# A new issue order table for a four-layer hybrid decoder trunk on one core

## The chip, the cores and the metric

The kernel runs on one core of one Trainium2 chip. The metric is the device time of one execution in microseconds (us), lower is better. Three executions of the kernel before took 2624.12, 2625.46 and 2626.32 us; the median is 2625.46.

## The reference: what is computed

Four layers on 1024 positions of width 1024, float32, causal. Each layer adds a gated branch to the stream x:

```python
for i in range(DEPTH):                       # DEPTH = 4
    mod = (c @ ada_w[i] + ada_b[i])[:, None, :]
    shift, scale, gate = jnp.split(mod, 3, axis=-1)
    h = rmsnorm(x, norm_g[i]) * (1.0 + scale) + shift
    y = (hgrn2_mixer, swa_mixer, gdn_mixer)[i % 3](h, ...)
    x = x + gate * y
```

Layers 0 and 3 are HGRN2 (a gated linear recurrence, 8 heads of 128), layer 1 is attention in a window of 128 positions (16 query heads of 64, 4 key heads, a learned sink per head, rotary angles), layer 2 is a gated DeltaNet. The DeltaNet projects h to q and k (8 heads of 128), v and z (16 heads of 128) and two decay columns; q, k and v go through a causal convolution of four taps and a SiLU; then comes a recurrence over chunks, in which each head keeps a 128 x 128 state S:

```python
X = triangular_solve(A + eye, rhs)           # A = (k*beta) k^T * decay, below the diagonal
u, w = X[..., :dv], X[..., dv:]
v_new = u - w @ S
o = (q * exp(d)) @ S + (q k^T * dec) @ v_new
S = S * exp(d_last) + (k * exp(d_last - d))^T @ v_new
```

Every mixer ends with a norm per head, a SiLU gate from z, and an output projection.

## The kernel before: tiles, stages and what sets the order

The layers follow each other in time: layer 0 to about 600 us, attention to about 1075, the DeltaNet to about 2050, layer 3 and the store to the end. The stream is held as 1024 channels (8 tiles of 128 partitions) by two halves of 512 positions.

**Projections.** All big products run in three passes of a split float32: weights and activations are each a high part and a remainder, and `mm3` (L346 ff.) issues hi x hi (L350), lo x hi (L351, activation remainder) and hi x lo (L352, weight remainder), 128 x 512 outputs each, 24 matmuls per projection tile. `load_w` brings a weight block by a DMA on SP's queue into a buffer of the tag "raw" (three of them), ScalarE casts the high part (L321, scaled L324), VectorE takes the remainder (L322, scaled L325). Projection tiles lie in a PSUM pool "proj" of two buffers, and a pool "ta" beside it.

**Conditioning.** The shift, scale and gate of the next layer are worked out as a side stream (`ada`, L574 to L602): blocks ada_w come by DMA into the same three raw buffers, VectorE multiplies and adds them into ada_acc (L574, L576), transposes (L594) and reduces it (L595), TensorE adds over partitions (L598), and VectorE adds the bias into mod (L602). What needs the next layer's h, or the attention's last part behind it on VectorE, comes after L602.

**Attention.** Per head group: transposes of q (qt_ps, L1609), a split of it (L1613 on ScalarE, L1614 on VectorE), scores (s_ps, L1624 to L1626), the softmax (L1628 to L1641 on VectorE), the product with v (L1653), the gate (L1593, L1659).

**DeltaNet.** Its heads go in eight units of one key head and two value heads each. For each projection tile `conv` (L811 to L833) has ScalarE read the PSUM tile twice, a plain copy (L820) and a copy scaled by one tap (L824), then three taps on VectorE (L826), a tanh on ScalarE and the last product on VectorE (L833). q and k are transposed (`trans`, L839, four matmuls into qtr_ps or ktr_ps) and their squares summed by four ScalarE reads of that (L846). z is gated on VectorE from PSUM (L917, L918). `inverse` makes the triangular inverse of a unit: kk and qk products (L937, L938), a substitution loop on VectorE (L973, L974), a transposed copy through memory (L979, L984, L985), products z_ps (L1002 to L1031). `scan` is the recurrence of a unit, eight steps one after the other. A step is

1. ks_ps (L1070, L1071): the state S against k and against q;
2. gd_y on VectorE (L1076), one per value head, and a scaled copy on ScalarE (L1077);
3. w_ps (L1081), one per head, and gd_ws on ScalarE (L1082);
4. S_ps (L1086), and the new state gd_S on VectorE (L1092);
5. gd_wg on ScalarE (L1096), w_ps again (L1097), and the output's sum on VectorE (L1100).

TensorE's part is short, and the steps wait for small results of the other engines. So the recurrence of one unit stands among projections, convolutions and the inverse of later units, from about 1235 to 1890 us. The DeltaNet's outputs are normed and sent out in `finish` (L1041 to L1055).

**What sets the order.** The program is written as generators that are woven together (`weave`), which fixes each instruction and what it depends on. What stands in which place of each engine's queue is then fixed by a table, ORDER: for TensorE, ScalarE, VectorE, SP and GpSimd a packed list of numbers, one per instruction, 14230, 2952, 5663, 1353 and 378 of them. `in_order`, called at the end of `trunk`, takes at each number n the n-th instruction that is still left in program order, and ties it behind the one taken before. Each engine's queue runs strictly in that order; between engines the true dependences hold.

Of the kernel before, what the change touches and what calls it, by code (L numbers as in the profile page):

```python
# [33 lines left out]
GB = {"k": 5, "q": 4, "kt": 4, "v": 4, "tmp": 2, "tb": 4, "of": 2, "f256": 4, "ot": 1}  # L34
# [22 lines left out]
        "iwx`sRaG)%n;9&`wg^-}vk$8Bfgq(0bLMh`yeg$%91-I{rUNP*(qh<haKcQxkV{%berc<`?^bC8mnktaaK)n6P-wjm0si<P%K!qk2Da%1?*4"
        "An?NWr!m2{}31KUZv=7zYm#0n7FkwWAJKJv<FU$*rR1Y$l&LkV(=fdH7&3R{-D?1%xkBgAe>EF{iV4cVksXahUemcK-DwyTEBfhHV|>b`*@h"
        "(v;AK47(7bq^Z2-|N-)iDKPJsYQoESY#w(6+4}`T+J!$L+1B)nMJTXniy^e24!WWepY@31A3StZI=YOPX^Q9V_^0$P(4b0^)G#ZEDhtQ2F_<"
        "cG=TpmAx$(I#m}#<uC}FZVC$letO2R2s1gZPXtdy2f<fwWt`WzVQp@badQg3y@7f$P=`;y-guJk)K>1Kutp?M$-Gq(~`{%lK>+t9r0A$p%`S"  # L60
        "-s9@MWRu3*lw@+(u9j@0qPsleHEZg&Sr=je={Q!-a4XNnf4%j&|X{h1^B_q@$(<Z@>MvIf;P1dtrWF{eFP1_<eW}?l}|OdmyJD@81uLu)r6$"
        "Zru1fa`oz6xC6HVzJ{c8d;%YT49a6~(eTxpO7Q_5-jjlVLOgo(C|x6%hdn$^(ly+>_c1(zpX2X2gll&{Jp`r)yc;rUq8Zf6$_l{J+R`tUK3I"
        "CJo>P_6wR{z!^G$|tUAuN|b#)a!f~Qa6i6KI%)o!`??6cj-vuEkYJCMr^&KZ^+Q#i%LhjR}e%+0~9<K85~Q<4i8E&yytPM<z=nlTkPJ39+I-"
        "(&#j-QQ+l7lMy>0!+iy6s4qMBu@&#x-7r5e0h19<ss~6MY04$7h1TA$4{QX@wMX*kHfL|5rDIZ-3;&DyO+J4IW_<3=cM*eK2?vNo_=!r!_#Y"
        "P_NSdg=;frHQ%H{H`v86h?`xIcm#W@>7tX^uKyjS0`vr3K3PO$i4aBco+)Rg3vM5?woKwkPWRP;qOUkNvLWiJj>qi{PzJfpxgOl<^qOY${Y}"
        "-D>Le~K&DpAlw2R7PkYQSi1m6(8|#}U6r*nJ3a@CgwoO+{MRyx<&s3V}(OVE&0vmYp`bNu@^dZ)|KVm2w6^W@f0|2~5-8?)a2_jC|A5(vr7W"
# [1728 lines left out]
```

## Time and profile before

| | |
|---|---|
| median of three executions | 2625.46 us (2624.12 to 2626.32) |
| the profiled execution | 2630.06 us |
| its span in the trace | 2628.4 us |
| mean granted TensorE clock | 0.988 |
| DMA | 312.07 MB, mean 119 GB/s |
| GpSimd's busiest group, sends of o_in (L1450) | 72 of 539 ns |

The page names engines PE (TensorE), PEld (its weight loads), DVE (VectorE), ACT (ScalarE), POOL (GpSimd) and SP. A group row gives line, engine, operation, output and inputs, count, busy time, mean of one, and the idle time before with its releaser. A wait row names who waited, at which line, for whose result; then us in all, times, and the longest. In a row of a stretch come its length, the busy time and the instructions of each engine, the granted TensorE clock (1.00 is full), the DMA share and GB/s. A 128 x 512 matmul is shown with a length of 0.39 us, but the next starts 0.23 us after it, since they overlap: so a busy share near 100% still holds short stalls, and they are read from the waits and the starts.

### The profile page before, as it was taken

The numbers are of one execution on the slowest core, as the hardware profiler recorded it, in microseconds if no ns is written. First come the engines' busy times: TensorE is split into PE (matmuls) and PEld (weight loads), VectorE is DVE, ScalarE is ACT, GpSimd is POOL, SyncE is SP. The second block draws the span as 40 slices with busy tenths as digits, with TensorE's granted clock in tenths as the row PEclk, the third lists the DMA queues.
The fourth block names the chain that finished last, engine by engine and source line by source line (L and its number), as shares of the span: only waits on it lengthen the run. The fifth ranks groups of instructions, "written<-read, shape, count | busy, mean of one in ns | idle before, by whom it ended". The sixth has DMA issues, their size and how long they took to land.

```text
span 2628.4 us, 50793 instructions
## 1 busy us (share of the span) xinstructions
PE 2542.7 (97%) x18271; PEld 2058.0 (78%) x18271; DVE 2014.9 (77%) x5663; ACT 1328.7 (51%) x3480; POOL 164.7 (6%) x382
## 2 busy tenths in 40 slices
PE   7999999999999999999999999999999999999999
PEld 4777887788988877787777788778788877788877
DVE  5585789886787868678889989888776846468775
ACT  4444344543465656455566666565644534344452
POOL 0001000001000000100011101100222000000000
PEclk8999999999999999999999999999999999999999
DMA  7333444644233343444344344333576412122443
GB/s 262 99 112 106 129 128 122 192 126 141 69 97 97 112 138 102 133 110 111 86 111 115 90 124 114 88 85 90 164 239 199 133 37 84 51 85 66 139 146 117
DMA packets 393618, 312.07 MB, mean 119 GB/s; under 512 B 74979, under 2 KB 320150, under 8 KB 393366
## 3 DMA queue, kind: packets, MB, share of 16 engines
q1 hardware_dynamic: 380822, 267.92, 34.5%
q0 software_dynamic: 12544, 40.90, 4.9%
q8 instruction: 144, 2.36, 0.4%
q14 instruction: 108, 0.88, 0.1%
HBM read 247.84 MB, written 60.88 MB: 117 GB/s over the span
## 4 chain that ended last, share of the span: by engine, by line
PE 80%; DVE 7%; DMA 6%; issue 4%; ACT 3%; SPq 0%; POOL 0%; DVEq 0%; ACTq 0%; POOLq 0%
PE proj_ps L350 12%; PE proj_ps L351 12%; PE proj_ps L352 12%; PE outp_ps L350 4%; PE outp_ps L351 4%; PE outp_ps L352 4%; PE projw_ps L352 2%; PE projw_ps L351 2%; PE projw_ps L350 2%; DMA ada_w<-in_ada_w_dram 2%; PE projt_ps L350 2%; PE projt_ps L351 2%; PE projt_ps L352 2%; PE lev_ps L1253 1%; PE pv_ps L1653 1%
## 5 line engine op out<-in xcount | busy, mean ns | idle before, releaser
L350 PE MATMUL proj_ps<-hhi,w_hi 128*128 128x512 f32 x1664 | 677.0, 407 | 16.4 <-ACT gd_tb L824 9.9
L352 PE MATMUL proj_ps<-hhi,w_lo 128*128 128x512 f32 x1664 | 673.4, 405 | 0.0
L351 PE MATMUL proj_ps<-hlo,w_hi 128*128 128x512 f32 x1664 | 672.1, 404 | 0.0
L350 PEld LDWEIGHTS proj_ps<-hhi,w_hi 128*128 128x128 f32 x1664 | 315.2, 190 | 80.2 <-ACT gd_tb L824 15.6
L352 PEld LDWEIGHTS proj_ps<-hhi,w_lo 128*128 128x128 f32 x1664 | 315.1, 189 | 58.2 <-issue 1.6
L351 PEld LDWEIGHTS proj_ps<-hlo,w_hi 128*128 128x128 f32 x1664 | 315.4, 190 | 56.7 <-issue 1.4
L321 ACT CAST w_hi<-w_raw 128x512 fp32r<-128x512 f32 x356 | 216.5, 612 | 266.2 <-PE proj_ps L351 150.9
L322 DVE TENSOR_TENSOR w_lo<-w_raw,w_hi 128x512 fp32r<-128x512 f32 x356 | 238.7, 675 | 129.6 <-ACT w_hi L321 124.0
L350 PE MATMUL outp_ps<-o_hi,w_hi 128*128 128x512 f32 x576 | 228.4, 398 | 1.6 <-ACT o_hi L1458 1.0
L351 PE MATMUL outp_ps<-o_lo,w_hi 128*128 128x512 f32 x576 | 229.5, 399 | 0.1
L352 PE MATMUL outp_ps<-o_hi,w_lo 128*128 128x512 f32 x576 | 228.8, 398 | 0.1
L324 ACT ACTIVATE w_hi<-w_raw,par 128x512 fp32r<-128x512 f32 (+1 forms) x136 | 94.5, 697 | 142.4 <-PE outp_ps L351 84.8
L826 DVE SCALAR_TENSOR_TENSOR gd_tb<-gd_xs,taps,gd_tb 128x512 f32<-128x512 f32 x192 | 146.0, 760 | 13.2 <-ACT gd_tb L824 12.4
L576 DVE SCALAR_TENSOR_TENSOR ada_acc<-ada_w,par,ada_acc 128x512 f32<-128x512 f32 x154 | 115.2, 748 | 35.1 <-DMA ada_w<-in_ada_w_dram 34.4
L350 PEld LDWEIGHTS outp_ps<-o_hi,w_hi 128*128 128x128 f32 x576 | 108.7, 189 | 25.0 <-issue 2.5
L325 DVE SCALAR_TENSOR_TENSOR w_lo<-w_raw,par,w_hi 128x512 fp32r<-128x512 f32 (+1 forms) x136 | 97.4, 718 | 39.9 <-ACT w_hi L324 39.5
L351 PEld LDWEIGHTS outp_ps<-o_lo,w_hi 128*128 128x128 f32 x576 | 108.9, 189 | 23.1 <-DVE o_lo L1459 1.5
L352 PEld LDWEIGHTS outp_ps<-o_hi,w_lo 128*128 128x128 f32 x576 | 108.9, 189 | 22.4 <-issue 0.9
L1450 POOL DMA_DIRECT2D o_in<-od x72 | 38.8, 539 | 1183.2 <-DVE sw_zs L1593 321.0
L350 PE MATMUL projw_ps<-w_hi,hhi 128*128 128x512 f32 x256 | 101.6, 402 | 2.4 <-DVE hg_q L1169 2.3
L351 PE MATMUL projw_ps<-w_lo,hhi 128*128 128x512 f32 x256 | 102.5, 402 | 0.0
L352 PE MATMUL projw_ps<-w_hi,hlo 128*128 128x512 f32 x256 | 102.4, 402 | 0.0
(431 smaller groups left out, 5386.3 us busy)
## 6 DMA issues: line engine op xcount, KB each, us to landing
ada_w<-in_ada_w_dram SPq DMA_DIRECT2D x160, 256.0 KB, 2.8
w_raw<-in_hg_in_w_dram SPq DMA_DIRECT2D x148, 256.0 KB, 2.9
w_raw<-in_gd_in_w_dram SPq DMA_DIRECT2D x128, 256.0 KB, 3.0
o_in<-od POOLq DMA_DIRECT2D x72, 256.0 KB, 3.6
x<-xd SPq DMA_DIRECT2D x64, 256.0 KB, 4.8
w_raw<-in_gd_out_w_dram SPq DMA_DIRECT2D x64, 256.0 KB, 3.2
xd<-x POOLq DMA_DIRECT2D x48, 256.0 KB, 2.7
w_raw<-in_sw_in_w_dram SPq DMA_DIRECT2D x44, 256.0 KB, 3.0
```

Of the source, the lines that this page charges most:

```text
L321: nc.scalar.copy(hi, raw)
L322: nc.vector.tensor_tensor(lo, raw, hi.bitcast(F32), ALU.subtract)
L324: nc.scalar.activation(hi, raw, AF.Copy, scale=scale)
L325: nc.vector.scalar_tensor_tensor(lo, raw, scale, hi.bitcast(F32), ALU.mult, ALU.subtract)
L350: mm(out, a[0], b[0], start=start, stop=False)
L351: mm(out, a[0], b[1], start=False, stop=False)
L352: mm(out, a[1], b[0], start=False, stop=stop)
L576: self.step = self.nc.vector.scalar_tensor_tensor(acc, w, c, acc, ALU.mult, ALU.add)
L826: last = nc.vector.scalar_tensor_tensor(y, xs[:, j:j + HT], w(j), y, ALU.mult, ALU.add)
L1253: return nc.tensor.matmul(pl[gs, n, c * 48:(c + 1) * 48], k[:, c * P + g * 32:c * P + (g + 1) * 32], x[:, 4 * c + g, :], start=True, stop= ...
L1450: nc.gpsimd.dma_start(t, od[(k0 + k) * P:(k0 + k + 1) * P, sl])
L1653: self.tied([lambda b=b, a=a: nc.tensor.matmul(po[a * 64:(a + 1) * 64], vg[:, n + 1 - nkb + b, :], p4s[b][:, :, a, :], start=b == nkb - 1, ...
```

## The change

Only ORDER changes. Its table is put together from three lists; attention and the DeltaNet come from one, made with longer PSUM reads on ScalarE. No instruction is added, taken away or given other operands. What stands at another place in its queue: 7636 of TensorE's 14230, 1368 of ScalarE's 2952, 3713 of VectorE's 5663, 482 of SP's 1353 and 38 of GpSimd's 378. In layer 0 the two sines of the rotary angles (L521, L522) now stand one behind the other on ScalarE; before, a sigmoid's tanh stood between them. With that, ScalarE's queue has six function table loads instead of eight.

The packed table is two source lines longer, so each line of code has a number higher by two than before (L1081 is L1083 after the change). The diff's first lines:

```diff
 ORDER = {
     "PE": (
...
-        "c-rlo>2nmv6~N!FW>>qqZwawlohu2nI*?!`ap*z<gySF)?1(!7a~KHm2jU2m3J`<{kV>4wI1q4Ta8+W5xSVoTlFzB6Dqr#~Uy}SM`INk)dv>"
...
+        "c-rln>u*%Y6~K?zcb_a~v9Z_24~$uZZ5BVkI6S=A=3y`x8!%5bL^PodX;DD}kq2o>fP_FEkdhEYp`oeNrfM6BR8=bFOWO}szf@{fsr}Z!rRO"
...
```

**TensorE, the recurrence of the fifth unit, seventh step.** In before its matmuls stand one behind the other. (w_ps_19608, S_ps_19654 and ks_ps_19718 belong to this step and to the start of the next; proj_ps is a projection.)

```order
L1086 MATMUL S_ps_19583<-gd_ws_19556,gd_kt_16936 128x256
L1097 MATMUL w_ps_19470<-gd_wg_19555,gd_uq_17631 128x128 x2
L1070 MATMUL ks_ps_19609<-gd_S_19585,gd_k_16846 128x256
L1071 MATMUL ks_ps_19609<-gd_S_19585,gd_q_17061 128x256
L1081 MATMUL w_ps_19608<-gd_y_19636,gd_uq_17631 128x128 x2
L1086 MATMUL S_ps_19654<-gd_ws_19643,gd_kt_16936 128x256
L1097 MATMUL w_ps_19608<-gd_wg_19642,gd_uq_17631 128x128
L1070 MATMUL ks_ps_19718<-gd_S_19656,gd_k_16846 128x256
L1071 MATMUL ks_ps_19718<-gd_S_19656,gd_q_17061 128x256
L1097 MATMUL w_ps_19608<-gd_wg_19642,gd_uq_17631 128x128
```

And with the change, from the step's second w_ps on:

```order
L1083 MATMUL w_ps_19608<-gd_y_19636,gd_uq_17631 128x128
L352 MATMUL proj_ps_19428<-hhi_12497,w_hi_19292 128x512
L353 MATMUL proj_ps_19428<-hlo_12498,w_hi_19292 128x512
L354 MATMUL proj_ps_19428<-hhi_12497,w_lo_19293 128x512
L1088 MATMUL S_ps_19654<-gd_ws_19643,gd_kt_16936 128x256
L1099 MATMUL w_ps_19608<-gd_wg_19642,gd_uq_17631 128x128
L352 MATMUL proj_ps_19428<-hhi_12497,w_hi_19292 128x512
L353 MATMUL proj_ps_19428<-hlo_12498,w_hi_19292 128x512
L354 MATMUL proj_ps_19428<-hhi_12497,w_lo_19293 128x512
L1072 MATMUL ks_ps_19718<-gd_S_19656,gd_k_16846 128x256
L1073 MATMUL ks_ps_19718<-gd_S_19656,gd_q_17061 128x256
L1099 MATMUL w_ps_19608<-gd_wg_19642,gd_uq_17631 128x128
```

Three projection matmuls now stand ahead of S_ps_19654 and three ahead of ks_ps_19718; between the two w_ps of gd_y there are five. The same is so in the third and the sixth unit, in one of two such steps of the last unit, and partly in the first. The first of the last unit's two stays as it was. The projection matmuls come from the middle of the same units, where fewer are left between a ks_ps and the next w_ps: in the third unit 16 in place of 39. On VectorE, between the state's update and gd_y of that middle step, there now stand 12 rows in place of 27 in the third unit, and 12 in place of 30 in the fifth.

**VectorE, the end of attention.** In before the last conditioning steps (ada_acc, ada_t, ada_red) stand among the gates of the last head groups and the weight splits.

```order
L576 SCALAR_TENSOR_TENSOR ada_acc_10807<-ada_w_11000,par_102,ada_acc_10807 128x512
L1659 TENSOR_TENSOR sw_of_10711<-pv_ps_10967,sw_zs_9748 128x2x128
L594 STREAM_TRANSPOSE ada_t_11003<-ada_acc_10807 128x512
L1593 SCALAR_TENSOR_TENSOR sw_zs_10720<-sw_tmp_10718,proj_ps_10640 128x512
L595 TENSOR_REDUCE ada_red_9728<-ada_t_11003 128x16
L322 TENSOR_TENSOR w_lo_11049<-w_raw_11047,w_hi_11048 128x512
L1593 SCALAR_TENSOR_TENSOR sw_zs_10638<-sw_tmp_10823,proj_ps_10734 128x512
L322 TENSOR_TENSOR w_lo_11055<-w_raw_11053,w_hi_11054 128x256
L322 TENSOR_TENSOR w_lo_11154<-w_raw_11152,w_hi_11153 128x512
L602 TENSOR_TENSOR mod_93<-ada_ps_11006,adab_107 32x12 x4
```

With the change they stand ahead of the last softmax rows (sw_st, sw_sm):

```order
L1643 TENSOR_SCALAR sw_sm_10883<-sw_sm_10883,sw_st_10852 128x256 x3
L578 SCALAR_TENSOR_TENSOR ada_acc_10807<-ada_w_10997,par_102,ada_acc_10807 128x512
L578 SCALAR_TENSOR_TENSOR ada_acc_10807<-ada_w_11000,par_102,ada_acc_10807 128x512
L596 STREAM_TRANSPOSE ada_t_11003<-ada_acc_10807 128x512
L597 TENSOR_REDUCE ada_red_9728<-ada_t_11003 128x16
L1639 TENSOR_TENSOR sw_st_10933<-sw_st_10933 128x4
L300 TENSOR_SCALAR rs_y_10544<-q_ms_10419 128x16
L1640 TENSOR_SCALAR sw_st_10933<-sw_st_10933 128x4
L302 SCALAR_TENSOR_TENSOR rs_t_10545<-rs_y_10544,q_ms_10419 128x16
L1641 RECIPROCAL sw_st_10933<-sw_st_10933 128x4
L303 TENSOR_TENSOR rs_t_10545<-rs_t_10545,rs_y_10544 128x16
```

mod (L602, now L604) still stands behind the split of w_lo_11154 (now L324), some twenty rows on. On SP, the x tiles of the next norm are now issued behind the ada_w blocks; before, they stood ahead of the last of them.

Elsewhere: in the DeltaNet the transposes of q and k (L839) stand one projection matmul earlier at nine of ten places where ScalarE's reads of them come right ahead of L824; at the tenth, at the start of the layer, a group of them moves so that five to six projection matmuls stand where none did. At the first query tile before the main loop, the ada_w step (L576) that stood ahead of L833 now stands behind L833 and L918, SP issues the inverse's loads (L985) ahead of that ada_w block, and a z_ps product (L1002) stands right behind the transposes of q. In the inverse the second z_ps products (L1012) have up to two projection matmuls less ahead of them, and the third (L1019) one or two more.

More of the change, by code (lines that the diff above doesn't have):

```diff
@@ L57 @@
[L57 to L66, printed above, removed]
@@ new lines @@
+        "IX#ZmI5C$+C6q&Xz0F)*arjcKlNpmJ#?dH4v7FRdt~Ilb_|+O{%fqOvNEI;{&q1)WM|;uaMY$J+!4YCbX5kmCOM<uc)>)kZD{+aQ0?X>rIY1"
+        ")aKkkQ_kb3p$OI4}1&@I{iZkrGifFS)}>wrxx?wx;XaZC>(*q^zR78QXEy=B5tTy7&Oy!d|mZ_X9f0e_|J(H"),
+    "Activation": (
+        "c-nndhnCwo3<R6HWK~P@`s}yfk}LoJe>VeC&Tj5ruujxSa5xx%D9a$Z&%770qSm&pG+WrRyhtxkQWQmre<E8ZLE`Jax2I%cI=nH~3jN@_%W{"
+        "!m3|>VGV(F=r!Z}>C5Ja3fn(+JP_LGxsvuiYIhN`bH!MU!)y0UZLDn6UDY#g~dZQt?oFoLh+9<0stc;^a}ODnpzF(R{@L`?iftdik6V}|MFF"
+        "w;gyz#qrMisNG(KRHo%X?z>6#w^(TDBq2o7_~Sm%jmw+mz%irb6`mSxdGSCJPq`>Vn9@3WftS{s*^ZvNC@Z<5y*4(A$Lr=R~2FJKzvTd&^aA"
+        "YmJDl$y9QJ1+G4)K%Yn+{&l!7cuhs2UT%sy87?C-|F7Bxqq#v=&Noi{^R>^mi2}RSk8BIdYOIczTHUq$_3<$&V1`+dp?;(v45Mf{X95#-|gd"
+        "%X_JR`0fZd?eU$hm?8;3>|*O5U5`J^2oFYY(?^06%l#yR}vIq91i<CJMi4sxitDyRgHMWCAEwgRm@;LbxGn8d1p4WsWNvv#wacct^=IMszPg"
+        "W580y*uWzrFG|TNimE8yVA7|Ul>0t#HPT(B8|T~?E#=gobR8u=&sBAGX&bY-C6zUe*lCeDr87U4DHk-|lKP{k3g6~=2YmTl!P~5`duqFB@my"
+        "IFr+x(6!21eI<dYxQ`W&^iB=N!+rF>6N$D()?O>-}_aHK(#_#vvi^)apVG7RABVP7k9=|deJLG4<-$D7;V;V)iK&^@D0>WYWF0`ZXnkt+MC5"
+        "d~WOxy$nt$;qI<@}oPzT&c;t_$SZndK}01X{?7O`J1NmiiDAUk6R4#5wriUWzBHE{-z@h=4x`y5E%1{VI~<lWnb5IR^c&6IW4jbKOZy5msMF"
+        "Jkag44{m}Ol>db9fuJUpX3Y&tPvuXO2<-9DHSlMRT6xt;rL-4*r^IGSEWUPmm>H<sJ9^sUaKH`H~&*y<4H8J%7aAawTJf4{7In?n9kf*L2<k"
+        "p9y9Lx(~O)~x%M}-#O&q1Ndav%%Do}h(J{OxvY__T-m3cHLlXz<5?CwW;Cw96&zdrN2o)Fhc_=0=%V%i?65XQU03(v!rtLH+5c8HmmT0^#i?"
+        "9H3?-Yq(tQ@p0eRZChW&Kf{{6#}fK@JWj8l;p5}uirTX()j?KW7Qk<)O@8|W7PUUInn0=I;=!gmTM~H(cV+qBoxoRr3#XslF{Zz82Oz%*>;G"
+        "^EG{WjV62}o`pkh?NhLxqz`IP-b3~NzKgeD!J9jD$|q0Ms!pFsBZ6WSiWL0i5i1EAgS_x9%dSH1u}0a1;tjmnna{V%LtL*|dFHrSM(%qaxd#"
+        "+#CjL%_Y&^2Q?xdnr$V-F9sQ&}=&7PsTuLxfk)|2PF-p#PvBqTbZ_L8chqT3&gM*DLa{1=YrJ`T2@;pZ&qGkwJ;j~Ry}2%;aSibo@_jZpZ!B"
+        ">404uIZD@{4tt(a?PuZf3l{U3f7=oBkIC$1t%u1CRaY;z1vG@^l!JD$=nGv-7N~imdh892xv%&ayuB4W$dG=f${_9#2uGn&EeKoP=3hs=yZ8"
+        "=Pu>TAR0Ha1*AsY>0}e;cm$VBy(td11q)jX*qg&_KDP|4HYkU$i6o-f*!YO5-KUz@$q19RIV0O5+XnsSRBme>7;n^S`3uO8&Ft(2W|@_P~fv"
+        "hz*x^R4njpxTO8wa52DN8m<dQ?6KjRm_cf+@<(6IqY)ww;n`<@w|@b!Lrfn"),
@@ new lines @@
+    "SP": (
+        "c-o~@=Wg3D5I!!6q%6zwkOS32Nk@{R2=X@%64WS)_Wj?YH)zRHT{J-MhjhI0@g@QOMOtf63jfI8zl?P@Lt-QRIp@G4Wyy>Dh%E}S091>P<>("
+        "s|k<de)Lzc~$_fWuChbm!FH&T&b4#^A{lX!~D<-^&tvbkw@hc3o0-m(!%ciH}!b$6e>Ja9@%DfllLV<wib-{Ays`tkD@{GJ%AE8O_3Ml>MP>"
+        "84d5_QzY~y1Tc8Hh?Q#mf9F=9o5`gj#_&^pSLJ*P19Jv8CqHNd`Uf{2861rHk%E!ZEx0Wx6b<Ja9|($IJ=@>Rk5C`UDw1hTwT{&XhtIwgV;%"
+        "%D8($&uy~#rV=zh2UFJXlLZ}&K1X6@>z6~HJkX$ngk+oXOsCWs5VF+ai#WQw_g#`ps2!Nq6HU>us3#RcBxecdV0zxcU^uV53ws4MFf(n{Iu>"
+        "Qu#DyWbm>O-1D#JeIe7burR19O?vWmzPlFh8GDQRd{wm04i-OT2B(GbWBpwH((qZ7-Ozs#mFoL*{&rGhbGIv0NtycrVe8@*ne_z8#|Qy)CW%"
+        "O!AWs%t$to;OPD>k$x2*4-84x^cuwdF?RhM^YQcjWA^pi)AQAJP4!UM6us;Zc*qyz"),
@@ L152 @@
     "Pool": (
[L153 to L154 removed]
+        "c-oDS3ktv>3_}w?^M~I5xNBu&>R>JqE05AfLBMQ;zuI+L2NFE!J#XgRAxh%8x0K?vk~0*bdRWdGOU{N`uS7$ns&IXgP8?wA8&$S1H!t6}X9T"
+        "+wVoXt-<%kF&ptY~hI01%Y0%!"),
 }
```

162 lines of the change are left out of this document (74 added, 88 removed).

## Prediction

> **What bounds the kernel now.** I read the page's span, busy times and chain first, then TensorE's busy time by stretches, then the waits of the one stretch that stands out, then single places on the timeline.
>
> The page:
>
> ```profile
> span 2628.4 us, 50793 instructions
> PE 2542.7 (97%) x18271; PEld 2058.0 (78%) x18271; DVE 2014.9 (77%) x5663; ACT 1328.7 (51%) x3480; POOL 164.7 (6%) x382
> PE 80%; DVE 7%; DMA 6%; issue 4%; ACT 3%; SPq 0%; POOL 0%; DVEq 0%; ACTq 0%; POOLq 0%
> ```
>
> TensorE carries 80% of the chain. A new issue order removes none of its matmuls, so it can only take out time in which TensorE stands, or runs at half clock. The stretches (attention, the gated DeltaNet's main loop, the last layer) show how much of that there is:
>
> ```profile
> core 0: us, PE busy (x) PEld busy (x) DVE busy (x) ACT busy (x) POOL busy (x), PEclk, DMA share, GB/s
> 600.00:1075.00 475.00, 466.83 (x3040) 390.68 (x3038) 376.12 (x1029) 255.58 (x617) 24.07 (x51) 0.99 0.35 109
> 1235.00:1890.00 655.00, 622.22 (x4518) 507.18 (x4517) 572.79 (x1643) 406.95 (x1289) 62.62 (x146) 0.99 0.39 104
> 2050.00:2565.00 515.00, 512.49 (x4316) 412.51 (x4315) 348.75 (x1104) 228.72 (x563) 10.78 (x20) 1.00 0.30 92
> ```
>
> The last layer leaves 2.5 us of 515 open, attention 8.2 of 475, the DeltaNet loop 32.8 of 655, so it is mostly there that an order can matter. VectorE is busy for 572.79 of the loop's 655 us (87%), against 68% in the last layer: that speaks against the change. TensorE's waits from 1075 to 1950 us, eight of its groups (us in all, times, longest):
>
> ```profile
> PE proj_ps L350 <- ACT gd_tb L824: 9.9, 10, 1.6
> PE proj_ps L350 <- DVE gd_tb L918: 4.8, 2, 2.4
> PE w_ps L1081 <- DVE gd_y L1076: 3.9, 5, 0.9
> PE S_ps L1086 <- ACT gd_ws L1082: 3.0, 6, 0.6
> PE w_ps L1097 <- ACT gd_wg L1096: 2.6, 6, 0.6
> PE w_ps L1081 <- ACT gd_ws L1082: 2.5, 5, 0.5
> PE ks_ps L1070 <- DVE gd_S L1092: 2.3, 3, 1.2
> PE qtr_ps L839 <- DVE gd_q L833: 1.5, 1, 1.5
> ```
>
> Two kinds: a projection that waits for its PSUM buffer until ScalarE's scaled copy of the convolution (L824) has read it, and the recurrence's short steps (L1070 to L1097), each of which needs a small VectorE or ScalarE result.
>
> **The recurrence.** How such a step looks where no projection stands between its matmuls, on TensorE's timeline (start, length, the wait in brackets):
>
> ```profile
> 1652.64 0.40 PE L352 MATMUL proj_ps<-hhi,w_lo 128*128 128x512 f32 x1
> 1653.03 0.70 PE L1086 MATMUL S_ps<-gd_ws,gd_kt 128*128 128x256 f32 x2
> ...
> 1654.56 0.49 PE L1097 MATMUL w_ps<-gd_wg,gd_uq 128*128 128x128 f32 x2 [0.61 <-ACT gd_wg L1096]
> ...
> 1656.39 0.49 PE L1081 MATMUL w_ps<-gd_y,gd_uq 128*128 128x128 f32 x2 [0.48 <-DVE gd_y L1076]
> 1657.40 0.46 PE L1081 MATMUL w_ps<-gd_y,gd_uq 128*128 128x128 f32 x2 [0.52 <-ACT gd_ws L1082]
> 1658.32 0.70 PE L1086 MATMUL S_ps<-gd_ws,gd_kt 128*128 128x256 f32 x2 [0.46 <-ACT gd_ws L1082]
> ...
> 1659.81 1.07 PE L1070 MATMUL ks_ps<-gd_S,gd_k 128*128 128x256 f32 x2 [0.57 <-DVE gd_tmp L973]
> ```
>
> Five waits of 0.46 to 0.61 us. In the order of before seven steps stand bare like this (one each in the third, fifth and sixth unit of eight, two each in the first and the last). In the changed order the three single ones have two to five projection matmuls between each pair, one of the last unit's is covered, and one of the first's about half: 4.5 of 7. How long such cover lasts is read off two projection matmuls in a row and the one that follows them:
>
> ```profile
> 1676.10 0.40 PE L351 MATMUL proj_ps<-hlo,w_hi 128*128 128x512 f32 x1
> 1676.34 0.39 PE L352 MATMUL proj_ps<-hhi,w_lo 128*128 128x512 f32 x1
> 1677.38 0.50 PE L350 MATMUL proj_ps<-hhi,w_hi 128*128 128x512 f32 x1 [0.66 <-ACT gd_tb L824]
> ```
>
> They start 0.24 us apart (0.23 over a longer run of them), so three give 0.68 us, more than any of the five waits. The five groups of such waits above (3.9, 3.0, 2.6, 2.5, 2.3) come to 14.3 us; 4.5/7 of it is **9.2 us gained**. The bounds are 0 (all of it returns behind VectorE) and 14.3.
>
> The cover is taken from the middle of the same units, and that is the edit's own cost. There a projection block filled the time from a step's first matmul until VectorE gave its result:
>
> ```profile
> 1449.87 0.59 PE L1070 MATMUL ks_ps<-gd_S,gd_k 128*128 128x256 f32 x2
> ```
>
> ```profile
> 1459.23 0.34 DVE L1076 SCALAR_TENSOR_TENSOR gd_y<-ks_ps,gd_ned,gd_v 128x128 f32<-128x128 f32 x1
> ```
>
> 9.4 us. In the changed order some 16 matmuls or 3.6 us of projections are left there, in five units. VectorE's list moves along: in the fifth unit 12 rows instead of 30 stand between the state's update (L1092) and that result. At the loop's mean of 572.79/1643 = 0.35 us, 12 rows are 4.2 us; with the result's own row I expect it some 4.5 us behind, a wait of about 0.9 us in each of the five units: **4.5 us lost**. Bounds: 0, and 9.4 − 3.6 = 5.8 us each if VectorE is no earlier than now.
>
> **The half clock.** The stretches in which the granted clock was 0.50 (four of the places, and the sum over all):
>
> ```profile
> 936.31:943.14 6.83, 6.74 (x24) 5.47 (x25) 5.80 (x14) 4.46 (x8) 2.54 (x5) 0.50 0.63 209
> 1223.03:1226.45 3.42, 3.42 (x10) 2.56 (x8) 3.21 (x10) 0.26 (x1) 1.70 (x3) 0.50 0.90 286
> 1284.47:1291.30 6.83, 6.31 (x16) 4.99 (x17) 5.79 (x19) 3.61 (x17) 0.00 (x0) 0.50 0.17 42
> 1659.94:1663.35 3.41, 3.41 (x10) 2.74 (x11) 2.31 (x8) 2.27 (x12) 0.00 (x0) 0.50 0.29 77
> 1881.81:1885.22 3.41, 3.41 (x12) 2.94 (x12) 1.31 (x3) 0.74 (x5) 1.06 (x2) 0.50 0.32 121
> sum 34.14, PE 33.53 PEld 27.39 DVE 26.60 ACT 15.39 POOL 6.57; mean PE 4.19 PEld 3.42 DVE 3.32 ACT 1.92 POOL 0.82
> ```
>
> 34.14 us at half clock hold 17.07 us of work, so 17.07 us are lost to it; the busy column hides that, since slow matmuls count as busy. The one at 1659.94 begins right after the bare step shown above, whose waits are 2.6 us in a stretch of 7. Those at 1284.47 and 1881.81 lie in bare steps too, 1223.03 follows the waits at 1219 and 1222, and 936.31 those at 934 and 936 below. Where the waits go, I take the half clock to go: half of the first unit's (1.7), the fifth unit's (1.7), one of the last unit's two (1.7), half of 1223's (0.9), 70% of 936's 3.4 (2.4): **8.4 us gained**. Bounds 0 and 17.07. Against it I put one new such stretch in a unit's middle, **1.7 us lost**. [...]
>
> **The convolution.** L824 reads PSUM right behind four small squares (L846) of transposes that stand late in a projection tile. In the changed order those transposes stand one projection matmul earlier at nine of the ten places (0.23 us each, 2.1), and at the tenth
>
> ```profile
> 1132.32 0.50 PE L350 MATMUL proj_ps<-hhi,w_hi 128*128 128x512 f32 x1 [1.55 <-ACT gd_tb L824]
> ```
>
> the cover grows from nothing to 1.33 us: **3.4 us gained** of the group's 9.9, with 0 and 9.9 as bounds. An earlier read on ScalarE can run into work before it there (ScalarE is busy 62% of the loop), hence nothing beyond the matmul's own 0.23.
>
> **1217 to 1222.** VectorE stands here for a conditioning weight, with the query's last convolution step (L833) behind it:
>
> ```profile
> 1217.92 0.75 DVE L576 SCALAR_TENSOR_TENSOR ada_acc<-ada_w,par,ada_acc 128x512 f32<-128x512 f32 x1 [0.90 <-DMA ada_w<-in_ada_w_dram]
> ```
>
> In the changed order that L576 comes behind L833 and L918, so 0.90 of waiting and about 0.7 of its own time leave the 1.5 us wait of the transposes: **1.6 us gained**, bounds 0 and 3.9 (with the 2.4 of L918's longer wait). SP's queue has the loads of the inverse (L985) ahead of this weight there, and a z_ps matmul now stands right behind the transposes; where its operand is late the gain is gone.
>
> **The end of attention.**
>
> ```profile
> 934.27 0.60 PE L1609 MATMUL qt_ps<-ident,sw_q 128*64 128x128 f32 x4 [1.68 <-DVE mod L602]
> 936.13 0.55 PE L1625 MATMUL s_ps<-kst,sw_qhi 128*128 128x128 f32 x2 [1.26 <-ACT sw_qhi L1613]
> ```
>
> ```profile
> 932.82 0.69 DVE L322 TENSOR_TENSOR w_lo<-w_raw,w_hi 128x512 fp32r<-128x512 f32 x1 [2.77 <-ACT w_hi L321]
> ```
>
> L602 stands behind this weight split, which waits for a weight that got its raw buffer late: the three raw buffers also hold the conditioning weights. In the changed order SP issues those ahead of the x tiles, and VectorE's last conditioning steps stand about twenty rows earlier, so a buffer comes free earlier. But L602 still stands behind the split. Of 1.68 + 1.26 I take **2.0 us gained**; bounds 0 and 2.9 (and a loss if VectorE, with those steps earlier, waits for their loads ahead of the softmax, below).
>
> **The small rest.** ScalarE reloads its function table twice less in layer 0, where the two sines now stand together:
>
> ```profile
> 202.20 1.28 ACT L522 ACT_TABLE_LOAD   x1
> ```
>
> ```profile
> PE lev_ps L1253 <- ACT hg_k L1174: 1.2, 1, 1.2
> ```
>
> ScalarE has slack, but this one wait of TensorE follows at 209 us: **0.6 us gained**, between 0 and 1.2. In the inverse the cover ahead of eight z_ps groups (L1012) shrinks by up to a matmul or two: **1.5 us lost** (0 to 8 × 0.46). The other moves of 7636 matmul places, in the HGRN2 layers above all, have no direction that I can read; I put **3 us lost**, an estimate from the open time of 8.2 and 2.5 us that attention and the last layer have now under such a table: a new one may leave some more. Between 3 gained and 6 lost.
>
> **The sum.** Gains 9.2 + 8.4 + 3.4 + 1.6 + 2.0 + 0.6 = 25.2; losses 4.5 + 1.7 + 1.5 + 3.0 = 10.7; net −14.5 us. The profiled execution took 2630.06 us, 4.6 above the median of the runs shown, 2625.46. From it: 2615.6 in the profiled kind of run, and **2611.0** as a median.
>
> **Rivals.** A measurement of this kernel tells about 0.2% (5.3 us) from no change, so "same" is 2620.2 to 2630.7.
>
> 1. VectorE sets the pace of the DeltaNet loop. Then each gap filled there opens elsewhere, and its own losses are part of that exchange. For: 87% busy, and 9.4 us for one result at 1449. Against: 82 us of it are idle, and most of the waits in the table are for ScalarE. What is left is attention's 2.0, its half clock's 2.4 and the table's 0.6: −5.0, **2620.5**. Chance 0.22.
> 2. The half clock doesn't follow the waits: its stretches stay or come elsewhere. Then the 8.4 and the 1.7 fall out: −7.8, **2617.7**. For it: steps with the same waits in the third unit had no half clock. Against: each of the eight stretches is near a stall. [...] Chance 0.12.
> 3. Slower: the middle of the units stands bare. If VectorE still needs 9.4 us for its result, five units wait 5.8 us (29.0), each long enough to bring a stretch of half clock (8.5); with the 25.2 gained and the other losses of 4.5: +16.8, **2642**. It decides where the result comes later than 6.0 us behind its first matmul (5 × (2.4 + 1.7) = 20.7, what is gained less the other losses). For: VectorE is nearly full. Against: its list has 12 rows there instead of 30. Chance 0.16.
>
> That the order isn't followed can't be: each engine's row is the table's.
>
> **How the numbers follow.** Forecast 0.50, of which 0.03 ends within the bound; rival 1 0.22 (0.08 faster, 0.14 same, since it lies at the edge), rival 2 0.12 (0.09 and 0.03), rival 3 0.16. Faster 0.47 + 0.08 + 0.09 = 0.64, same 0.20, slower 0.16. The likeliest case alone spans 2599 to 2620. The range runs from the gains without the losses (−25.2, with the 1.5 that attention and the table may add: 2599) to 2632, which takes in rivals 1 and 2 and a rival 3 only just past its point of decision; beyond lies most of rival 3, and below little.
>
> **What would show it.** Right: in the fifth unit's last steps no wait over 0.3 us and no half clock at the unit's end; half-clock time down from 34 to about 20 us; the L824 group at 6 to 7 us; w_ps waits of about 1 us in the units' middle. Wrong: the five recurrence groups together not under 10 us (rival 1), half clock still at 30 us or more with the waits gone (rival 2), waits for gd_y of 2.4 us or more in the middle of units (rival 3).

## The result, and the profile after

Six executions of the changed kernel took 2605.68 to 2618.30 us, median **2609.2**; six of the kernel before beside it 2624.12 to 2632.04, median 2626.18. The ratio is 0.993 (95% interval 0.9913 to 0.9948), a gain of 17 to 18 us; 2611.0 was forecast. In a later comparison, on another set of executions, the same kernel had 0.9938 (0.9919 to 0.9956). The profiled execution took 2616.35 us (span 2614.7, mean clock 0.990), one of the slower of its six. One execution in the experiments below, of the kernel with the DeltaNet alone, ran at a granted clock of 0.653 and took 3555 us; it is left out of every figure.

The page of the changed kernel, same lines as before:

```profile
span 2614.7 us, 50796 instructions
PE 2536.9 (97%) x18271; PEld 2055.2 (79%) x18271; DVE 2015.1 (77%) x5663; ACT 1327.7 (51%) x3478; POOL 161.5 (6%) x382
PE 80%; DVE 8%; DMA 5%; issue 3%; ACT 2%; POOL 0%; SPq 0%; DVEq 0%; POOLq 0%; ACTq 0%
```

VectorE's and ScalarE's work is what it was; the span is 13.7 us shorter. TensorE's row for the main loop, from the loop's first matmul to the first behind it, before and after:

```profile
1235.16:1890.27 655.11, 622.33 (x4518) 507.29 (x4517) 572.63 (x1643) 406.95 (x1289) 62.82 (x147) 0.99 0.39 104
```

```profile
1235.80:1877.77 641.97, 616.66 (x4511) 503.66 (x4506) 572.98 (x1644) 409.11 (x1288) 60.76 (x148) 0.99 0.41 106
```

The loop is 13.1 us shorter, nearly the whole difference of the two profiles. Length less TensorE's busy time is 32.8 us before and 25.3 after: 7.5 us of waiting are gone. The other 5.6 are busy time: 18.7 us of the loop ran at half clock before and 10.2 after, which makes about 4 of them; what the rest is stays open. VectorE does the same 573 us of work in the shorter loop, 89% of it in place of 87: it was not the limit.

TensorE's waits from 1060 to 1950 us after the change (code lines are two higher):

```profile
PE proj_ps L352 <- ACT gd_tb L826: 7.0, 11, 1.2
PE w_ps L1083 <- DVE gd_y L1078: 3.8, 3, 1.4
PE vtr_ps L841 <- DVE gd_tb L835: 2.6, 4, 1.0
PE z_ps L1004 <- ACT gd_Tc L986: 2.3, 1, 2.3
...
PE ks_ps L1072 <- DVE gd_S L1094: 1.7, 4, 0.8
...
PE S_ps L1088 <- ACT gd_ws L1084: 1.3, 3, 0.5
...
PE w_ps L1099 <- ACT gd_wg L1098: 0.7, 1, 0.7
...
PE w_ps L1083 <- ACT gd_ws L1084: 0.5, 1, 0.5
```

The five groups of the recurrence come to 8.0 us in place of 14.3. The step of the fifth unit that stood bare, on TensorE's timeline after the change:

```profile
1651.39 0.39 PE L1083 MATMUL w_ps<-gd_y,gd_uq 128*128 128x128 f32 x2
...
1652.77 0.38 PE L1083 MATMUL w_ps<-gd_y,gd_uq 128*128 128x128 f32 x2
...
1653.69 0.62 PE L1088 MATMUL S_ps<-gd_ws,gd_kt 128*128 128x256 f32 x2
...
1655.10 0.67 PE L1072 MATMUL ks_ps<-gd_S,gd_k 128*128 128x256 f32 x2
```

No row has a wait any more; where "..." stands, projection matmuls run. Half clock in the changed kernel's profile (three of its places in the DeltaNet, and the sum of all six):

```profile
1225.21:1232.04 6.83, 6.83 (x125) 5.03 (x125) 6.05 (x14) 3.44 (x10) 2.50 (x4) 0.50 0.40 134
1286.65:1290.06 3.41, 3.12 (x8) 2.60 (x9) 2.74 (x10) 2.67 (x15) 0.00 (x0) 0.50 0.29 77
1870.33:1877.16 6.83, 6.33 (x17) 5.11 (x18) 4.67 (x11) 4.05 (x15) 2.85 (x6) 0.50 0.60 203
sum 30.72, PE 29.78 PEld 24.05 DVE 25.05 ACT 17.82 POOL 7.72; mean PE 4.96 PEld 4.01 DVE 4.18 ACT 2.97 POOL 1.29
```

It is gone at 1660, where the covered step is, and at 1780, but the sum is 30.7 in place of 34.1 us, not the 20 that was expected, and just past the 30 that the prediction named as the sign of its second rival. One profile each can't settle that, since the sum differs from run to run; the experiments do.

**A measure that helps.** Time times mean granted clock takes off half of every stretch at half clock; it is called time at full clock here, and the rest, time x (1 − clock), the half-clock part. It serves to compare kernels and is not the true cost of half clock: in the first profile of before 12 of some 30 us of that part lie in the first 63 us, and the 6.83 us of half clock at the end of attention cost about 1 us at most, where the part says 3.4 (below). The clock is on record to 0.001, which is 2.6 us. In 11 of the 15 sets of executions time at full clock varies less than the time does, in four more. For the kernel before, 30 executions beside the second set of experiments give 2599.9 + 29.1 us, 11 beside the last set 2598.7 + 31.3; for the changed kernel two sets of six give 2586.1 + 24.8 and 2586.1 + 27.0. So by this measure the gain is about 13 us of waits and about 4 us of half clock.

### The profile page after: what moved, and what is told of

Its sections match the earlier page's. It is cut to its first block, busy times and chain, and to the rows that moved or that the text cites. A ratio compares the mean times of both kernels' runs of the same rounds, so it can differ in the third digit from the quotient of the medians.

```text
span 2614.7 us, 50796 instructions
## 1 busy us (share of the span) xinstructions
PE 2536.9 (97%) x18271; PEld 2055.2 (79%) x18271; DVE 2015.1 (77%) x5663; ACT 1327.7 (51%) x3478; POOL 161.5 (6%) x382
## 4 chain that ended last, share of the span: by engine, by line
PE 80%; DVE 8%; DMA 5%; issue 3%; ACT 2%; POOL 0%; SPq 0%; DVEq 0%; POOLq 0%; ACTq 0%
PE proj_ps L352 12%; PE proj_ps L353 12%; PE proj_ps L354 12%; PE outp_ps L353 5%; PE outp_ps L354 5%; PE outp_ps L352 5%; PE projw_ps L353 2%; PE projw_ps L354 2%; PE projw_ps L352 2%; PE projt_ps L353 2%; PE projt_ps L354 2%; PE projt_ps L352 2%; DMA ada_w<-in_ada_w_dram 1%; PE lev_ps L1255 1%; DMA o_in<-od 1%
## 5 line engine op out<-in xcount | busy, mean ns | idle before, releaser
L324 DVE TENSOR_TENSOR w_lo<-w_raw,w_hi 128x512 fp32r<-128x512 f32 x356 | 238.8, 674 | 153.3 <-ACT w_hi L323 151.4
```

What stands on the lines that cost most here:

```text
L324: nc.vector.tensor_tensor(lo, raw, hi.bitcast(F32), ALU.subtract)
```

## The experiments

In the kernels below lines have before's numbers unless the changed kernel itself is meant. An order is put together from the two tables: which instructions belong to a stretch is decided by their start in before's trace, on all queues at once, and inside a stretch they keep the order of the one or the other kernel.

The last two columns are means over the executions.

| kernel | median us | ratio to before (95%) | mean time at full clock | before's, same set |
|---|---|---|---|---|
| DeltaNet alone | 2617.3 | 0.9945 (0.9930 to 0.9959) | 2589.9 | 2599.8 |
| attention alone | 2628.7 | 0.9994 (0.9984 to 1.0004) | 2600.5 | 2599.8 |
| five stretches of the loop | 2634.4 | 1.0020 (1.0012 to 1.0029) | 2604.2 | 2599.8 |
| DeltaNet without those | 2631.7 | 1.0006 (0.9997 to 1.0015) | 2603.5 | 2599.8 |
| 1629 to 1758 us alone | 2621.3 | 0.9969 (0.9958 to 0.9980) | 2593.8 | 2599.9 |
| DeltaNet without that | 2618.3 | 0.9960 (0.9946 to 0.9975) | 2595.9 | 2599.9 |
| transposes 1 earlier | 2630.0 | 0.9999 (0.9988 to 1.0011) | 2599.2 | 2599.9 |
| transposes 3 earlier | 2633.0 | 1.0010 (0.9999 to 1.0021) | 2603.5 | 2599.9 |
| changed kernel again | 2612.6 | 0.9938 (0.9919 to 0.9956) | 2586.1 | 2598.7 |
| changed, two steps bare | 2619.0 | 0.9955 (0.9938 to 0.9971) | 2591.6 | 2598.7 |
| changed, conditioning later | 2617.8 | 0.9956 (0.9940 to 0.9973) | 2587.2 | 2598.7 |

**Which layer.** The changed order in one part, that of before in the rest:

```diff
-all five queues, 1070 to 2050 us: order of before
+all five queues, 1070 to 2050 us: changed order
```

> The order of before, with the changed order in the DeltaNet alone (what started from 1070 to 2050 us in before's trace, on all five queues). Theory of the prediction: the gain lies here, in the recurrence's steps and what follows from them; against before -12 to -16 us. Rival that the gain is spread over all layers: -5 to -8. Rival that the gain is only the place at which half clock falls by chance: the time lies between before and after with a half-clock sum in the trace that explains all of the difference.

Measured: −14.5 us (−18.4 to −10.8), of which 9.9 at full clock. The DeltaNet carries it, as the first theory said. The profiles of the two whole kernels agree (each was profiled twice, see below): from the DeltaNet's first transposes of q (qtr_ps) to the first lev_ps of layer 3, before takes 1016.0 and 1017.2 us, the changed kernel 1003.9 and 1000.1.

```diff
-all five queues, 600 to 1070 us: order of before
+all five queues, 600 to 1070 us: changed order
```

> The order of before, with the changed order in attention alone (600 to 1070 us). The prediction's terms: -2.0 for the two waits at its end and -2.4 for the half clock behind them, about -4. Rival, from the trace of after, where attention is 2.5 us later at 930 us and gets 2 us back by 1064: 0 within 1.5 us, with the half clock of 6.83 us at its end still there.

Measured: nothing (+0.7 at full clock, within the interval). The rival was right about attention's waits: what the prediction gained at the end of attention is lost elsewhere in it (below). In this execution the half clock at its end didn't come at all, though it came again with the same waits in others. It hardly mattered: from the first qt_ps to the DeltaNet's first qtr_ps attention takes 399.5 and 399.6 us in the two profiles of before, both with 6.83 us at half clock; in the changed order it takes 399.7 and 400.4 with them (the changed kernel, and the one with two bare steps) and 399.4 and 399.3 without (the changed kernel's second profile, and attention alone). So at this place half clock cost about 1 us at most, and not 3.4.

**Which part of the DeltaNet.** First, five stretches cut out round the bare steps, and their complement:

```diff
-1268-1292, 1436-1478, 1629-1666, 1711-1759, 1852-1900 us: order of before
+the same stretches: changed order
```

> The order of before, with the changed order in five stretches of the DeltaNet's main loop alone, the middle and the end of the units with bare steps (1268 to 1292, 1436 to 1478, 1629 to 1666, 1711 to 1759, 1852 to 1900 us), 188 of 655 us. Theory of the prediction: recurrence -9.2, half clock -5.1 there, +6.2 for the units' middles, about -8 against before. Rival that VectorE sets the pace: 0 to -3, with the waits back elsewhere in the loop. Rival that the convolution and the rest of the loop carry the gain: 0 to -3 here and the gain in the kernel with the other stretches.

> The counterpart: the changed order in the DeltaNet (1070 to 2050 us) without those five stretches, which keep the order of before. Theory of the prediction: convolution -3.4, the place at 1217 -1.6 and half of its half clock -0.9, z_ps +1.5, about -4 against before. Rival that the convolution carries the gain: -8 or more. Rival that the new waits outside the stretches cancel the convolution's: 0 within 2.

Both came out slower, +4.4 and +3.7 us at full clock, and both theories missed. The profile of the first shows why it did, on VectorE and then on TensorE:

```profile
1443.86 0.19 DVE L973 TENSOR_TENSOR gd_tmp<-gd_A,gd_Tb 128x31 f32<-128x31 f32 x1 [6.92 <-DMA gd_A<-ablk]
```

```profile
1445.78 0.79 PE L1081 MATMUL w_ps<-gd_y,gd_uq 128*128 128x128 f32 x2 [6.24 <-DVE gd_y L1076]
```

At the cut at 1436 some rows of VectorE's two lists stand about fifteen places apart. The stretch put the inverse's loop ahead of the recurrence's results; its loads had not landed, VectorE stood for 6.9 us, and gd_y and TensorE stood behind it. What cost the second kernel its 3.7 us was not followed up. This tells nothing of the bare steps, but it shows how closely the five lists of one table hang together. So a piece was taken at whose ends nearly the same instructions have been issued in both orders:

```diff
-1629 to 1758 us: order of before
+1629 to 1758 us: changed order (449 places on TensorE, 298 on VectorE, 166 on ScalarE, 36 on SP)
```

> The order of before, with the changed order in one piece of the main loop alone, from the middle of the fifth unit to the end of the sixth unit's steps (1629 to 1758 us, a fifth of the loop); at both ends nearly the same instructions have been issued in both orders, so that the seams leave no work behind, as they did in the kernel with five stretches. Theory: the piece holds two of the seven bare steps (waits of 2.6 and 1.6 us) and saves about 6 us of TensorE's idle time, plus or minus 3 us of half clock, so -4 to -9 against before. Rival that VectorE sets the pace: idle time unchanged within 2 us, 0 to -2.

> The counterpart: the changed order in the whole DeltaNet (1070 to 2050 us) but for that piece, which keeps the order of before. Theory: the rest of the DeltaNet's gain, -4 to -9 against before, and with the piece alone it comes to about the -14.4 of the whole DeltaNet. Rival that the gain needs one unbroken list: 0 here.

Measured −8.1 (interval −11.0 to −5.3) and −10.5 us (−14.2 to −6.6); at full clock −6.1 and −4.0, together −10.1 against the −9.9 of the whole DeltaNet. A fifth of the loop, with two bare steps, carries more than half of the gain at full clock, in the size expected. Its profile shows where: from the fifth unit's first ks_ps to the seventh's, the two profiles of before take 187.8 and 185.6 us, of which TensorE stands 11.5 and 10.7; here it is 178.5 and 7.2. That is 4 us of standing, where 6 were expected. By time the two pieces come to more than the whole (−18.6 against −14.5), at full clock they add up; in either case the rival of one unbroken list, 0 for the second, falls.

**The cover itself.** In the changed kernel, on TensorE alone, the projection matmuls inside two steps are put ahead of the step (rows of the fifth unit):

```diff
+L351..L351 MATMUL proj_ps_19428 x11
 L1081 MATMUL w_ps_19608
-L351, L352, L350, L351, L352 MATMUL proj_ps_19428
 L1081 MATMUL w_ps_19608
-L350, L351, L352 MATMUL proj_ps_19428
 L1086 MATMUL S_ps_19654
 L1097 MATMUL w_ps_19608
-L350, L351, L352 MATMUL proj_ps_19428
 L1070 MATMUL ks_ps_19718
```

> The changed kernel with the cover of two steps taken away on TensorE alone: in the fifth and the sixth unit the 11 and 14 projection matmuls between the matmuls of the seventh step are put ahead of the step, so that it stands bare; the other four queues are as changed. Theory: the waits of a bare step come back, 2.6 and 1.6 us in before, less up to 1 us for the wait for gd_y ahead of it that the matmuls now cover: +3 to +5 against the changed kernel, half clock aside. Rival that VectorE sets the pace: within 1 us of the changed kernel.

Measured beside the changed kernel: 2619.0 against 2612.6, 5.5 us at full clock, plus or minus about 3, a little more than expected. TensorE's timeline in the fifth unit's bared step, and the granted clock behind the two:

```profile
1648.88 0.49 PE L1081 MATMUL w_ps<-gd_y,gd_uq 128*128 128x128 f32 x2 [0.46 <-ACT gd_ws L1082]
1649.83 0.70 PE L1086 MATMUL S_ps<-gd_ws,gd_kt 128*128 128x256 f32 x2 [0.46 <-ACT gd_ws L1082]
...
1651.31 0.90 PE L1070 MATMUL ks_ps<-gd_S,gd_k 128*128 128x256 f32 x2 [0.57 <-DVE gd_S L1092]
```

```profile
1651.62:1655.03 3.41, 3.41 (x11) 2.69 (x10) 2.75 (x10) 3.07 (x13) 0.00 (x0) 0.50 0.29 77
1743.78:1747.19 3.41, 3.41 (x10) 2.75 (x10) 2.31 (x9) 2.62 (x11) 0.00 (x0) 0.50 0.18 53
```

The waits are back (1.5 us in this step, 1.8 in the sixth unit's), and with each step a stretch of half clock right behind it; neither is in the two profiles of the changed kernel. VectorE's, ScalarE's and the DMA queues' orders are untouched, so it is the cover on TensorE that does it, and not VectorE's pace. What was not tried: TensorE's changed order with before's lists on the other engines, and a cover for the step of the first unit that stays bare; no run shows what either would do.

**Does half clock follow the waits?** The two kernels once more, unaltered:

```diff
 ORDER unchanged
```

> The changed kernel once more, unaltered, for a second profile and for its time beside the two kernels below. If half clock follows the waits, its stretches stand at the same places as in the first profile of it (1095, 1225, 1287, 1870 us in the DeltaNet); if the place in a grid of 3.41 us decides as well, some of them go and others come, at the same waits. Time against before: -17 by the first comparison.

> The kernel before once more, for a second profile. Same question: half clock at 1223, 1284, 1660, 1779, 1882 and 1889 us again (it follows the waits), or at other stalls of the same order (the place in the grid decides too). Theory: 1223 and 1284 again, where the waits are longest, the others by chance; sum between 80 and 2590 us between 17 and 41.

In the second profile of the kernel before the fifth unit's step stands bare with the same waits (to 0.01 us; three of the five are shown):

```profile
1656.88 0.49 PE L1097 MATMUL w_ps<-gd_wg,gd_uq 128*128 128x128 f32 x2 [0.61 <-ACT gd_wg L1096]
...
1660.65 0.70 PE L1086 MATMUL S_ps<-gd_ws,gd_kt 128*128 128x256 f32 x2 [0.46 <-ACT gd_ws L1082]
...
1662.14 0.67 PE L1070 MATMUL ks_ps<-gd_S,gd_k 128*128 128x256 f32 x2 [0.57 <-DVE gd_tmp L973]
```

but half clock came not there, where the first profile had it, but at the third unit's step, where the first had none:

```profile
1469.36:1476.19 6.83, 6.14 (x17) 4.82 (x17) 5.88 (x18) 3.52 (x16) 0.10 (x1) 0.50 0.16 41
1659.94:1663.35 3.41, 2.30 (x11) 1.44 (x10) 2.77 (x11) 2.64 (x14) 0.00 (x0) 1.00 0.01 4
```

So the waits alone do not settle it here. In the loop half clock came with bare steps: in five profiles with before's order there (the two of that kernel, attention alone, both kernels with earlier transposes) each stretch of it but those at 1780 stands at a bare step. Whether a given step had it differed from one execution to the next. In the first profiles of the two kernels every stretch at half clock that ends within the profile is 3.41 us long or two to four times that, and their starts lie whole multiples of 3.413 us apart (1284.47 and 1659.94 in before: 375.47 us, 110 of them). In the second profile of before they lie elsewhere: from 1284.47 in the first to 1469.36 in the second are 184.89 us, 54.2 of them. These are the intervals of that spacing at the fifth and the third unit's step, in the first profile and then in the second:

```profile
1656.53:1659.94 3.41, 1.86 (x9) 1.29 (x10) 2.71 (x11) 2.59 (x10) 0.00 (x0) 1.00 0.24 74
1465.38:1468.80 3.42, 1.99 (x9) 1.15 (x7) 3.10 (x11) 2.82 (x10) 0.00 (x0) 1.00 0.58 170
```

```profile
1657.10:1660.51 3.41, 2.09 (x10) 1.28 (x9) 3.18 (x12) 1.96 (x9) 0.00 (x0) 1.00 0.48 126
1465.95:1469.36 3.41, 1.70 (x8) 0.92 (x7) 2.78 (x10) 2.72 (x10) 0.00 (x0) 1.00 0.48 135
```

TensorE was busy for 1.86 and 1.70 us of the two intervals that half clock followed, and for 1.99 and 2.09 us of the two that it did not. Busy time does not settle it either: in the changed kernel's profile full clock followed the first of these two rows, with 1.82 us, and half clock the second, with 2.14:

```profile
1218.38:1221.80 3.42, 1.82 (x10) 1.04 (x8) 1.56 (x3) 2.19 (x10) 0.00 (x0) 1.00 0.58 104
1221.80:1225.21 3.41, 2.14 (x68) 1.95 (x69) 3.06 (x8) 2.59 (x8) 2.02 (x3) 1.00 1.02 286
```

Why the same step had half clock in one execution and not in the next, no run shows.

In the five profiles half clock came at the first unit's step in five of five, at the third's in four, at the fifth's in two. From 1070 to 1950 us it sums to 23.9, 30.7, 13.7, 30.7 and 17.1 us in those, and to 20.5, 13.7 and 3.4 with the changed order there (the changed kernel twice, DeltaNet alone): 23.2 against 12.5 in the mean, of which half, 5 us, would be time.

**The convolution.** On TensorE alone, ten groups of transposes of q are moved up; with one matmul, for instance:

```diff
 L351 MATMUL proj_ps<-hlo,w_hi 128x512
-L352 MATMUL proj_ps<-hhi,w_lo 128x512
 L839 MATMUL qtr_ps<-ident,gd_q 128x128 x4
+L352 MATMUL proj_ps<-hhi,w_lo 128x512
```

> The order of before, with ten groups of four transposes of q (L839) one projection matmul earlier on TensorE, and nothing else. Theory: the ten waits for the convolution's scaled copy (9.9 us) shrink by up to 0.23 each, to about 7.8, so -2 against before, half clock aside. Rival: ScalarE or VectorE is not there earlier, the transposes or the squares wait, and the group stays at 9 to 10 us: 0.

> The same with the ten groups three projection matmuls earlier than in before. Theory: up to 0.69 us less for each wait, to about 4 us in all, -5 to -6 against before, if the transposes' input (L833 on VectorE) is there; rival: the input is late, waits of the transposes for L833 take the place of the convolution's, sum of both groups at 9 us or more: 0 or slower.

Measured: no difference for one (−0.7 at full clock), and 3.6 us more at full clock for three. The waits of each:

```profile
PE proj_ps L350 <- ACT gd_tb L824: 8.6, 10, 1.6
```

```profile
PE proj_ps L350 <- ACT gd_tb L824: 7.0, 7, 1.9
...
PE qtr_ps L839 <- DVE gd_q L833: 3.5, 7, 1.1
```

One matmul takes 1.3 of the 9.9 us, three take 2.9, but then the transposes wait 3.5 us for VectorE's product in place of 1.5. For three the rival holds: the next thing that is late is L833, seven times and by up to 1.1 us. The two groups together still fall, from 11.4 to 10.5 us, so why the kernel is slower at all stays open.

**The end of attention.** In the changed kernel, on VectorE alone, the conditioning steps that stand ahead of softmax rows go behind them:

```diff
-L578 ada_acc_10807<-ada_w_10988
 L1630 sw_st_10933 ... L1643 sw_sm_10883 x3
+L578 ada_acc_10807<-ada_w_10988, ada_w_10991, ada_w_10994
-L578 ada_acc_10807 x2, L596 ada_t_11003, L597 ada_red_9728
 L1639 sw_st_10933 ... L1643 sw_sm_10955 x4
+L578 ada_acc_10807 x2, L596 ada_t_11003, L597 ada_red_9728
```

> The changed kernel with the last seven conditioning steps of attention (L578 three times, then L578 twice, L596, L597) put behind the softmax rows that they stand ahead of, on VectorE alone. Theory: the two waits of pt_ps at 920 and 929 us (1.0 and 0.85) go, and the wait for mod (0.9) grows back towards the 1.7 of before, since the raw buffers come free later: -1 plus or minus 1 against the changed kernel, half clock aside. Rival that the conditioning steps have nothing to do with those waits: pt_ps still waits 1.8 in all.

Measured: 2617.8 against 2612.6 (1.1 us more at full clock, the rest half clock), the wrong sign. The profile puts it in attention: 402.7 us from the first qt_ps to the first qtr_ps, against 399.7 and 399.4. In the changed kernel TensorE has two new waits there, and the rows of VectorE and ScalarE behind them are these:

```profile
919.91 0.30 PE L1649 MATMUL pt_ps<-ident,sw_sm 128*128 128x128 f32 x1 [0.99 <-DVE sw_st L1634]
928.84 0.66 PE L1649 MATMUL pt_ps<-ident,sw_sm 128*128 128x128 f32 x4 [0.85 <-ACT sw_pth L1652]
```

```profile
915.87 0.75 DVE L578 SCALAR_TENSOR_TENSOR ada_acc<-ada_w,par,ada_acc 128x512 f32<-128x512 f32 x1 [1.67 <-DMA ada_w<-in_ada_w_dram]
```

```profile
927.31 0.99 ACT L323 CAST w_hi<-w_raw 128x512 fp32r<-128x512 f32 x2 [3.90 <-DMA w_raw<-in_sw_out_w_dram]
```

With the steps later, the first wait is gone and the second grows (TensorE, then ScalarE):

```profile
930.73 1.12 PE L1647 MATMUL pt_ps<-ident,sw_sm 128*128 128x128 f32 x4 [4.07 <-ACT sw_pth L1650]
```

```profile
929.27 0.92 ACT L321 CAST w_hi<-w_raw 128x512 fp32r<-128x512 f32 x2 [6.90 <-DMA w_raw<-in_sw_out_w_dram]
```

So there are two causes. The wait at 920 is the conditioning step that stands for its load ahead of a softmax row. The one at 929 is ScalarE's: with the changed order two weight casts stand ahead of the copy of the softmax's transposes (L1652), and they wait for loads into raw buffers that the conditioning steps free. Steps later mean buffers later (SP issues these loads at 925.6 us in place of 921.4), casts later, and 4.1 us for TensorE. The expectation had the buffers' delay in mind for mod alone, which still waits 0.9 us, and missed the casts.

## Why the prediction was right, step by step

**The time** (2611.0 against 2609.2, −14.5 forecast and −17 measured) and the place are right. The sizes, from the profiles and the parted kernels:

- **Recurrence, 9.2 gained:** right. The waits in the bare steps come to 14.1 us before (3.0, 2.9, 2.6, 1.6 and 4.0 in the five places) and to 6.1 after (1.7, 0.3, none, none and 4.1), so 8.0, and the bared steps give 5.5 back for two of them. The last unit, of whose two steps one was taken as covered, gained nothing. The forecast read 14.3 off five groups that hold 1.3 us of waits elsewhere and lack 1.1 us of the bare steps; that evens out.
- **The units' middle, 4.5 lost and 1.7 of half clock:** failed. No wait for gd_y stands in the middle of the third to the sixth unit. With twelve rows in place of some thirty VectorE starts it 3.3 us behind ks_ps in the fifth unit (1640.23 and 1643.54), where the forecast had put 4.5 and before took 9.3, so it came in time for the shorter cover. New are waits of 1.0 us at 1263 and 1.4 at 1919, in the first and the last unit: 2.4 us, whose cause no run shows. The third of that group, 1.4 us at 1868, lies in the last unit's bare steps and is counted above.
- **Half clock, 8.4 gained less 1.7:** the sign right, and 3.41 us of half clock came back behind each of the two bared steps; the size was too large: about 4 us over the whole kernel by the executions' clocks, about 5 in the DeltaNet by the profiles. The failing step was to take each half-clock stretch of one profile as fixed to its stall, where in five profiles it came at the first unit's step five times, at the third's four and at the fifth's twice, and to count each at half its length: for the 2.4 at the end of attention there was about 1 us at most to be gained.
- **Convolution, 3.4:** the group fell nearly as forecast, from 9.9 to 7.0, but the time did not follow: alone it is worth 0.7 or nothing, and in the changed kernel the transposes of v wait 2.6 us for VectorE in place of 0.2.
- **1217 to 1222, 1.6:** 1.1 (waits of 1.5 and 2.4 before; 0.6, and 2.3 for z_ps, after). The price named for z_ps came up in full.
- **Attention, 2.0:** failed. The wait for mod fell from 1.7 to 0.9, but the waits of pt_ps took 1.8 (2.6 in the second profile): the loss that was put in a bracket, and the casts that were not seen.
- **The rest, 0.6 gained, 1.5 and 3 lost:** the wait behind the table loads (1.2 us before) is gone. The z_ps groups wait 8.1 us in place of 6.5, of which 2.3 is the one at 1223 counted above. In the HGRN2 layers 3 lost was put. The whole gains 12.6 to 13.7 us at full clock, the DeltaNet 9.9, attention none, which leaves them some 3 gained, plus or minus 2; the profiles show less. Layer 0, to the first qt_ps, takes 692.3 and 690.0 us before and 692.1 and 690.2 after, layer 3, from its first lev_ps, 520.5 and 519.0 before and 519.0 and 518.8 after. No run parted those layers.

So the place and the main term were right, but that the sum came within 2 us is in part luck: the terms that came out too high (half clock, convolution, attention) were about as much as losses that did not come in full (the units' middle, the HGRN2 layers). What has a row or a run, 8.0 + 4.5 + 1.1 + 0.7 − 2.4, comes to about 12 of the 17 us. Of the rivals the first, VectorE as the pace, falls by the bared steps and by the loop's rows. The third, late results in the middle, never arose. The second was half right: with the two steps bared half clock came back behind both, but in before the fifth unit's step had it in one profile and not in the other, at the same waits.

## What to carry to other kernels

Where a short chain of dependent steps on several engines runs beside a long stream of matmuls, spread the stream so that each link has more work behind it than the latency of its reply (here 0.68 us against 0.46 to 0.61); here two steps bared cost 5.5 us at full clock, and in their profile 3.41 us of half clock stood behind each. The issue order here was one object over all queues: transposes moved on TensorE alone gained nothing (0.7 us less at full clock for one matmul, 3.6 more for three), and a piece cut where VectorE's lists differed by some fifteen places cost 4.4 us at full clock. Compare time at full clock beside time: it helps to part a change of a few microseconds from the chance of half clock, but at the end of attention it takes 3.4 us of half clock for lost time, where about 1 us at most was lost.

## What the runs showed that was not expected

- The same program with the same waits ahead of it got half clock at 1660 us in one execution and at 1469 in the next. Over six executions of the changed kernel the mean clock ran from 0.987 to 0.993 and the time from 2618.3 to 2605.7 us.
- Half clock of 6.83 us at the end of attention made that layer about 1 us longer at most.
- Half clock of 3.41 us came back behind each of two steps when their cover was taken away, with waits of only 0.46 to 0.74 us in them.
- A conditioning step on VectorE that comes later held up TensorE by 4.1 us over four stations: a raw buffer, a load, a cast on ScalarE (6.9 us), and a copy behind the cast.
